# Up-projection of a transformer trunk in seven products: their order, their PSUM banks and what is tied behind the bank reads

## The chip, the cores and the metric

The kernel runs on one core of one Trainium2 chip. The metric is the device time of one execution in microseconds, smaller is better; a time given for a kernel is the median of its runs. PE is the matrix engine, PEld its weight loads, DVE the vector engine, ACT the scalar (activation) engine, POOL the GpSimd engine, SP the engine that issues almost all DMAs. Each engine takes its instructions strictly in order.

## The reference, cut to what matters

```
h = rmsnorm(x, norm_ffn[l]) * (1.0 + sc_f) + sh_f
gate, up = jnp.split(h @ w_up[l], 2, axis=-1)
x = x + g_f * ((jax.nn.silu(gate) * up) @ w_down[l])
```

This is the feed-forward part of the one layer, all in fp32; x is 2048 tokens by 1024, w_up is 1024 by 2 x 2816. Before it stand the mixer with its in- and out-projection, after it the last RMSNorm. The change touches the product `h @ w_up` and the `silu(gate) * up` on its results.

## The kernel before, in words

Every matrix product is done on fp32 operands that are split into a high and a low part (`split`, L151 and L152): ACT casts the high part, DVE subtracts it from the source to get the low one. One product of a 128x128 weight tile and 512 tokens then is three matmuls (`mm3`, L173 to L175).

The up-projection takes tokens in two halves b of 1024, and the 22 units of 128 gate and 128 up columns in 11 pairs. That makes 22 passes, called pairs here. For one unit and one token half the product is a 2x2 block product (gate and up columns by two halves of the contraction, times two token quarters of 512), which is done by Strassen's method in Winograd's form: seven products P1 to P7 in place of eight. Each of the seven has a left operand (A11, A12, A22 of the weights, or the sums S1 to S4 of them, `LEFT`) and a right one (B11, B21, B22, or the sums T1 to T4 of the activations, `RIGHT`). A product is 4 contraction tiles x 3 matmuls = 12 matmuls per unit, so a pair issues 7 x 2 x 12 = 168, the stage 22 x 168 = 3696.

- **Weights.** `Up.__init__` loads a unit's raw weights in two DMAs (`load_raw`, L158) into a pool of 4 slots, so two units fill it. `Up.weights` splits A11, A12, A22 into slots w (6) and S1 to S4 into slots x (4); the sums are made on POOL in place (L571, L572, L575, L581).
- **Activations.** The right operands of one token half stand split in 14 panel slots; those of the second half are loaded and split during the last pair of the first half (`Panel`, L534).
- **Banks.** PSUM has eight banks, a ring of one tag. A unit takes four of them: a (P1, then P2 added on it), d (P5, then P3), b (P6), c (P7, then P4). A pair thus goes once around the ring. The partial sums are read midway: ACT copies a after P1 (u, L604); DVE adds b to u (L607), c to u and d to that (c22, L611 and L612) after P7, before P4 goes onto c; Silu reads a after P2 (L616); then g1 (L620, L621) and c22 (L624, L626) are finished.
- **Results.** Four result blocks of a pair are combined on POOL (L637 to L646) and stored to DRAM (`put` in `sums`, L634) for the down-projection.
- **Background.** In the first token half `ffn_inputs` makes the activations of the second half (POOL, ACT, DMAs), in the second half `down_sums` makes the sums of the down weights (loads L498, POOL L507 to L515, stores L502).

The order on each engine is set by a scheduler that sends out what is ready by the order of the code; a load or store stands on SP at the place the scheduler gave it, and a store that waits for its data holds all loads behind it. `tc.issue_after(ins)` lets instructions be placed only behind `ins`.

Of the kernel before, what the change touches and what calls it, by code (L numbers as in the profile page):

```python
# [13 lines left out]
P = 128  # L14
# [8 lines left out]
NB = 2  # L23
# [19 lines left out]
def trunk_kernel(  # L43
# [408 lines left out]

    def ffn_inputs(b):


        def put(name, kt, t):
            nc.sync.dma_start(hd[b][name][:, kt, :], t)

        def get(i, kt):
            t = tmp(f"b_{b}_{i}_{kt}")  # L460
            nc.sync.dma_start(t, xd[b][kt // 2][:, 2 * (kt % 2) + i, :])
            nc.gpsimd.tensor_mul(t, t, rs[i])  # L462
            nc.scalar.activation(
                t, t, AF.Identity, bias=mod[:, 24 + kt:25 + kt], scale=gain[:, 1, kt:kt + 1]
            )
            return t

        rs = [tmp(f"r_{b}_{i}") for i in range(QB)]
        for i in range(QB):
            nc.sync.dma_start(rs[i], rd[b][i])  # L470
        yield
        for kt in range(4):
            b11 = get(0, kt)
            put("B11", kt, b11)
            t1 = get(1, kt)
            yield
            nc.gpsimd.tensor_sub(t1, t1, b11)
            put("T1", kt, t1)
            t2 = get(1, kt + 4)
            put("B22", kt, t2)  # L480
            yield
            nc.gpsimd.tensor_sub(t2, t2, t1)
            put("T2", kt, t2)
            b21 = get(0, kt + 4)
            put("B21", kt, b21)
            yield
            nc.gpsimd.tensor_sub(b11, t2, b11)
            put("T3", kt, b11)
            nc.gpsimd.tensor_sub(b21, b21, t2)
            put("T4", kt, b21)  # L490
            yield

    def down_sums():

        def get(p, name):
            t = tmp(f"{name}_d{p}")
            u = U_FF + 3 * (2 * p + int(name[2]) - 1) + 2
            nc.sync.dma_start(t, wts[u][:, 512 * (int(name[1]) - 1):][:, :512])  # L498
            return t

        def put(p, name, t):
            nc.sync.dma_start(sd[p][:, ("S2", "S1", "S4", "S3").index(name), :], t)  # L502

        for p in range(NPR):
            a21, a22, a11 = [get(p, n) for n in ("A21", "A22", "A11")]
            yield
            nc.gpsimd.tensor_add(a21, a21, a22)  # L507
            put(p, "S1", a21)
            nc.gpsimd.tensor_sub(a11, a21, a11)
            put(p, "S2", a11)  # L510
            nc.gpsimd.tensor_sub(a22, a22, a11)
            put(p, "S3", a22)
            a12 = get(p, "A12")
            yield
            nc.gpsimd.tensor_sub(a12, a12, a11)  # L515
            put(p, "S4", a12)
            yield

    ORDER_UP = ("P1", "P2", "P5", "P6", "P7", "P4", "P3")
    ORDER_DOWN = ("P1", "P6", "P7", "P4", "P5", "P3", "P2")

    class Panel:
# [5 lines left out]
        def load(self, name, k):  # L530
            t = panel(f"{name}_{self.b}_{k}", [P, 2, 2, Q])
            for i in range(2):
                raw = tmp(f"raw_{name}_{self.b}_{k}_{i}")
                nc.sync.dma_start(raw, hd[self.b][name][:, 2 * k + i, :])  # L534
                split(t[:, i], raw)
            self.t.setdefault(name, []).extend([t[:, 0], t[:, 1]])

        def steps(self):
            for p in ORDER_UP:
                for k in range(2):  # L540
                    self.load(RIGHT[p], k)
                    yield

        def product(self, p):
            for k in range(2):
                self.load(RIGHT[p], k)

    class Up:
# [18 lines left out]
        def weights(self, p):  # L567
            a11, a12, a21, a22 = self.rg[:, :512], self.rg[:, 512:], self.ru[:, :512], self.ru[:, 512:]
            if p == "P1":
                self.put("A11", a11)  # L570
                nc.gpsimd.tensor_add(a21, a21, a22)  # L571
                nc.gpsimd.tensor_sub(a11, a21, a11)  # L572
            elif p == "P2":
                self.put("A12", a12)
                nc.gpsimd.tensor_sub(a12, a12, a11)  # L575
            elif p == "P5":
                self.put("S1", a21)
            elif p == "P6":
                self.put("S2", a11)
            elif p == "P7":  # L580
                nc.gpsimd.tensor_sub(a21, a22, a11)  # L581
                self.put("S3", a21)
            elif p == "P4":
                self.put("A22", a22)
            else:
                self.put("S4", a12)

        def product(self, p):
            n = f"{self.b}_{self.j}"
            bank = {"P1": "a", "P2": "a", "P5": "d", "P3": "d", "P7": "c", "P4": "c", "P6": "b"}[p]  # L590
            first = p in ("P1", "P5", "P7", "P6")
# [8 lines left out]
            getattr(self, "after_" + p, lambda: None)()  # L600
# [27 lines left out]
    def up(b, t, step, after=lambda p: None):  # L628

        def sums(pair, us):
            def put(name, g):
                nc.sync.dma_start(gd[pair][name][:, b, :], g)  # L634

            (b11, t1), (b21, b22) = [(u.g1, u.c22) for u in us]
            nc.gpsimd.tensor_sub(t1, t1, b11)  # L637
            t2 = tmp(f"t2_{b}_{pair}")
            nc.gpsimd.tensor_sub(t2, b22, t1)
            put("B11", b11)  # L640
            put("B21", b21)
            put("B22", b22)
            put("T1", t1)
            put("T2", t2)
            nc.gpsimd.tensor_sub(b11, t2, b11)
            nc.gpsimd.tensor_sub(b21, b21, t2)  # L646
            put("T3", b11)
            put("T4", b21)

        for pair in range(NPR):  # L650
            us = [Up(b, 2 * pair + k, t) for k in range(2)]
            for p in ORDER_UP:
                for u in us:
                    u.weights(p)
            if pair:
                step()
            for p in ORDER_UP:
                for u in us:
                    u.product(p)
                if pair == NPR - 1:  # L660
                    after(p)
            if pair < NPR - 1:
                sums(pair, us)
        return lambda: sums(pair, us)

    def down(ready):
# [38 lines left out]
        ready()  # L705
# [223 lines left out]
    g = panels[0].steps()  # L929
# [3 lines left out]
    g = ffn_inputs(1)  # L933

    def step():
        finish_rms()
        next(g, None)
        next(g, None)

    ready = up(0, panels[0].t, step, panels[1].product)  # L940
    ready()
    g = down_sums()
    next(g)
    next(g)
    down(up(1, panels[1].t, stepper(g, 4)))
# [62 lines left out]
```

## Time and profile before

| | us |
|---|---|
| runs (3) | 2088.53, 2089.32, 2092.90 |
| median | 2089.32 |
| profiled execution | 2091.01 |
| its span, first to last instruction | 2089.3 |
| PE busy | 1972.1 (94%) |
| DVE busy | 1219.9 (58%) |
| ACT busy | 743.2 (36%) |
| POOL busy | 644.9 (31%) |
| mean granted TensorE clock | 0.974 |

The up-projection stands from 698.4 to 1633.9 us of the span. A matmul that runs at half the clock counts as busy all its time, so 94% busy is not 94% of full speed. The granted clock is 1.00 at 2.4 GHz and 0.50 at 1.2 GHz. Times of the rows are microseconds from the start of the span unless a unit stands with them.

### The profile page before, as it was taken

The page shows a single profiled execution, that of the slowest core. Times are in us where ns is not written, and L with a number is a line of the kernel's source. Part 1 is how long each engine was busy: PE and PEld are TensorE (multiplying, and loading weights), DVE is VectorE, ACT ScalarE, POOL GpSimd, SP SyncE. Part 2 cuts the span into 40 slices and gives each one's busy share as a digit, 9 for nine tenths or more (in the row PEclk, how much of TensorE's full clock was granted, in tenths as well). Part 3 has the DMA queues.
Part 4 walks back from the last instruction along what each step waited for, and adds up shares of the span by engine and source line. Part 5 has one row for each costly group of instructions (what it writes and reads, how often), then busy time and mean ns, then how long its engine had stood idle before and what let it go on. Part 6 is the DMA issues. An engine that isn't in the chain of part 4 may idle for free.

```text
span 2089.3 us, 23165 instructions
## 1 busy us (share of the span) xinstructions
PE 1972.1 (94%) x8424; PEld 1595.7 (76%) x8424; DVE 1219.9 (58%) x1683; ACT 743.2 (36%) x1228; POOL 644.9 (31%) x440
## 2 busy tenths in 40 slices
PE   5999998999999799999999898897999999999996
PEld 3778876888888577888887776786788888888874
DVE  7987677434475656646656764445555464444464
ACT  3431666223474432333334332222232242243321
POOL 3100044012310345466563445555452100010110
PEclk9999999999999899999999999999999999999998
DMA  8467244423456433343435444444343684234432
GB/s 280 169 216 268 101 166 147 133 79 121 156 203 193 153 116 111 138 165 112 143 140 195 137 157 159 155 167 139 122 171 132 262 331 157 91 117 151 136 116 81
DMA packets 136918, 328.23 MB, mean 157 GB/s; under 512 B 14305, under 2 KB 22497, under 8 KB 134498
## 3 DMA queue, kind: packets, MB, share of 16 engines
q1 hardware_dynamic: 136802, 326.74, 45.3%
q8 instruction: 66, 1.08, 0.2%
q14 instruction: 50, 0.41, 0.1%
HBM read 242.28 MB, written 84.41 MB: 156 GB/s over the span
## 4 chain that ended last, share of the span: by engine, by line
PE 63%; DMA 6%; DVE 6%; issue 3%; POOL 3%; ACT 2%; SPq 1%; DVEq 0%; POOLq 0%; ACTq 0%
PE d_P L174 7%; PE d_P L173 6%; PE d_P L175 6%; PE gu_c L173 3%; PE gu_c L174 3%; PE gu_c L175 3%; PE gu_d L174 3%; PE gu_d L173 3%; PE gu_d L175 3%; PE gu_a L173 2%; PE gu_a L175 2%; PE gu_a L174 2%; DMA raw_gu<-in_wts 2%; PE c L173 2%; PE c L175 2%
## 5 line engine op out<-in xcount | busy, mean ns | idle before, releaser
L152 DVE TENSOR_TENSOR A<-raw_gu,A 128x512 fp32r<-128x512 f32 x132 | 128.2, 994 | 228.7 <-ACT A L151 228.2
L152 DVE TENSOR_TENSOR ws<-raw_gu,ws 128x512 fp32r<-128x512 f32 x176 | 171.5, 1008 | 38.9 <-ACT ws L151 36.6
L151 ACT CAST A<-raw_gu 128x512 fp32r<-128x512 f32 x132 | 79.2, 618 | 276.7 <-PE gu_c L175 203.3
L151 ACT CAST ws<-raw_gu 128x512 fp32r<-128x512 f32 x176 | 102.4, 619 | 184.4 <-PE gu_d L175 67.9
L173 PE MATMUL gu_a<-B,A 128*128 128x512 f32 x352 | 138.9, 395 | 15.4 <-ACT u L604 15.4
L175 PE MATMUL gu_a<-B,A 128*128 128x512 f32 x352 | 138.2, 393 | 0.0
L174 PE MATMUL gu_a<-B,A 128*128 128x512 f32 x352 | 137.9, 392 | 0.0
L175 PE MATMUL c<-h,w_c 128*128 128x512 f32 x320 | 125.7, 393 | 4.8 <-DVE w_c L152 4.8
L133 POOL TENSOR_TENSOR sf<-sf,sq 128x512 f32<-128x512 f32 x18 | 28.3, 1576 | 328.7 <-ACT sq L132 327.7
L173 PE MATMUL c<-h,w_c 128*128 128x512 f32 x320 | 126.1, 394 | 0.7 <-DVE ya L301 0.7
L174 PE MATMUL c<-h,w_c 128*128 128x512 f32 x320 | 125.5, 392 | 0.3 <-DVE h L224 0.3
L173 PE MATMUL gu_c<-T,A 128*128 128x512 f32 x176 | 76.8, 436 | 42.8 <-DVE c L611 42.7
L637 POOL TENSOR_TENSOR c<-c,g 128x512 f32<-128x512 f32 x22 | 29.3, 1332 | 265.2 <-DVE c L626 265.2
L571 POOL TENSOR_TENSOR raw_gu<-raw_gu 128x512 f32<-128x512 f32 x44 | 61.8, 1405 | 153.3 <-DMA raw_T<-hd_T 99.9
L173 PE MATMUL d_P<-T_d,S_d 128*128 128x512 f32 x264 | 102.7, 389 | 0.0
L174 PE MATMUL d_P<-T_d,S_d 128*128 128x512 f32 x264 | 102.7, 389 | 0.0
L175 PE MATMUL d_P<-T_d,S_d 128*128 128x512 f32 x264 | 102.7, 389 | 0.0
L462 POOL TENSOR_TENSOR b<-b,r 128x512 f32<-128x512 f32 x32 | 41.7, 1318 | 178.5 <-DMA b<-xd 143.9
L133 POOL TENSOR_TENSOR sx<-sx,sq 128x512 f32<-128x512 f32 x14 | 21.0, 1499 | 233.2 <-ACT sq L132 232.3
L173 PEld LDWEIGHTS gu_a<-B,A 128*128 128x128 f32 x352 | 66.7, 190 | 30.7 <-ACT u L604 16.4
L152 DVE TENSOR_TENSOR S_d<-raw_S_d,S_d 128x512 fp32r<-128x512 f32 x44 | 32.1, 734 | 93.8 <-ACT S_d L151 87.1
L173 PEld LDWEIGHTS gu_c<-T,A 128*128 128x128 f32 x176 | 36.9, 209 | 55.8 <-DVE c L611 47.5
(256 smaller groups left out, 5642.1 us busy)
## 6 DMA issues: line engine op xcount, KB each, us to landing
raw_gu<-in_wts SPq DMA_DIRECT2D x88, 512.0 KB, 4.8
raw_T_d<-gd_T SPq DMA_DIRECT2D x44, 512.0 KB, 4.1
raw_B_d<-gd_B SPq DMA_DIRECT2D x33, 512.0 KB, 3.4
wm<-in_wmodT SPq DMA_DIRECT2D x32, 512.0 KB, 4.3
raw_o<-in_wts SPq DMA_DIRECT2D x32, 512.0 KB, 5.5
raw_c<-in_wts SPq DMA_DIRECT2D x28, 512.0 KB, 4.0
gd_B<-g SPq DMA_DIRECT2D x44, 256.0 KB, 2.0
gd_T<-g SPq DMA_DIRECT2D x44, 256.0 KB, 2.0
```

The source lines that it names most:

```text
L133: (add or nc.vector).tensor_add(acc, acc, sq)
L151: nc.scalar.copy(dst[:, 0, :], src)
L152: (sub or nc.vector).tensor_sub(dst[:, 1, :], src, dst[:, 0, :].bitcast(F32))
L173: nc.tensor.matmul(ps, l_hi, r_hi, start=start, stop=False, skip_group_check=onto)
L174: nc.tensor.matmul(ps, l_hi, r_lo, start=False, stop=False, skip_group_check=onto)
L175: nc.tensor.matmul(ps, l_lo, r_hi, start=False, stop=stop, skip_group_check=onto)
L462: nc.gpsimd.tensor_mul(t, t, rs[i])
L571: nc.gpsimd.tensor_add(a21, a21, a22)
L637: nc.gpsimd.tensor_sub(t1, t1, b11)
```

## The change

The seven products come in the order P1, P5, P6, P2, P7, P3, P4, with the operands and matmuls as they were. A unit takes three banks: a (P1, P6, P7 and P4 added onto one another), d (P5, P3) and e (P2). Each partial sum is read between two products onto its bank: ACT copies a after P1 (s), d after P5 (c22), a after P6 (u); DVE adds e to s after P2 and a to c22 after P7; d is added to u after P3, and a is multiplied by s after P4.

The raw loads of the next pair stand in one block; its splits are tied, by `issue_after`, behind the bank read of the current pair's product, one product later than their own place, and the last ones (A22) behind the pair's own P1. Stores of results, of the activations' and the weights' sums are collected (`Late`, `Pair.stores`) and tied behind the last load issued. The panels of the second half are loaded four blocks at a time and split one product later. The steps of the background work come after P6 and P3 of each pair.

```diff
+    class Late:
+        def put(self, dst, t):
+            self.stores.append((dst, t))
+        def flush(self):
+            with tc.issue_after(last["load"]):
+                for dst, t in self.stores:
+                    nc.sync.dma_start(dst, t)
+            self.stores = []
...
-    ORDER_UP = ("P1", "P2", "P5", "P6", "P7", "P4", "P3")
+    ORDER_UP = ("P1", "P5", "P6", "P2", "P7", "P3", "P4")
...
         def steps(self):
             for p in ORDER_UP:
-                for k in range(2):
-                    self.load(RIGHT[p], k)
-                    yield
+                self.load(RIGHT[p])
+                yield
+                self.split(RIGHT[p])
+                yield
...
-            bank = {"P1": "a", "P2": "a", "P5": "d", "P3": "d", "P7": "c", "P4": "c", "P6": "b"}[p]
-            first = p in ("P1", "P5", "P7", "P6")
+            bank = {"P5": "d", "P3": "d", "P2": "e"}.get(p, "a")
+            first = p in ("P1", "P5", "P2")
...
         def after_P1(self):
-            self.u = tmx(f"u_{self.b}_{self.j}")[:, :Q]
-            nc.scalar.copy(self.u, self.ps["a"])
+            self.s, ins = self.copy("s", "a")
+            return ins
+        def after_P5(self):
+            self.c22, ins = self.copy("c22", "d")
+            return ins
         def after_P6(self):
-            nc.vector.tensor_add(self.u, self.ps["b"], self.u)
+            self.u, ins = self.copy("u", "a")
+            return ins
+        def after_P2(self):
+            nc.vector.tensor_add(self.s, self.ps["e"], self.s)
+            return nc.scalar.activation(self.s, self.s, AF.Silu).ins
         def after_P7(self):
-            self.c22 = tmx(f"c22_{self.b}_{self.j}")[:, :Q]
-            nc.vector.tensor_add(self.c22, self.ps["c"], self.u)
-            nc.vector.tensor_add(self.c22, self.ps["d"], self.c22)
-        def after_P2(self):
-            self.s = tmp(f"s1_{self.b}_{self.j}")
-            nc.scalar.activation(self.s, self.ps["a"], AF.Silu)
-        def after_P4(self):
-            self.g1 = tmp(f"g1_{self.b}_{self.j}")
-            nc.vector.tensor_add(self.g1, self.ps["c"], self.u)
-            nc.vector.tensor_mul(self.g1, self.g1, self.s)
+            return nc.vector.tensor_add(self.c22, self.ps["a"], self.c22).ins
         def after_P3(self):
             nc.vector.tensor_add(self.u, self.ps["d"], self.u)
             nc.scalar.activation(self.u, self.u, AF.Silu)
-            nc.vector.tensor_mul(self.c22, self.c22, self.u)
+            return nc.vector.tensor_mul(self.c22, self.c22, self.u).ins
+        def after_P4(self):
+            return nc.vector.tensor_mul(self.s, self.ps["a"], self.s).ins
...
+    def ups(panels, begin, backgrounds):
+        todo = [(b, p) for b in range(NB) for p in range(NPR)]
+        pair, before = begin, None
+        for n, (b, p) in enumerate(todo):
+            after = Pair(*todo[n + 1], panels[todo[n + 1][0]].t) if n + 1 < len(todo) else None
+            bg = backgrounds[b]
+            due = pair.due
+            for k, prod in enumerate(ORDER_UP):
+                ins = pair.product(prod)
+                with tc.issue_after(ins):
+                    if k == 0 and due:
+                        pair.weights(due)
+                    if k and after:
+                        after.weights(ORDER_UP[k - 1])
+                if p == NPR - 1 and b + 1 < NB:
+                    if k:
+                        panels[b + 1].split(RIGHT[ORDER_UP[k - 1]])
+                    panels[b + 1].load(RIGHT[prod])
+                elif p == 0 and b and k == 0:
+                    panels[b].split(RIGHT[ORDER_UP[-1]])
+                if before:
+                    if k == 0:
+                        before.sums()
+                    if k == 3:
+                        with tc.issue_after(last["load"]):
+                            before.stores()
+                    if k == 5:
+                        with tc.issue_after(last["load"]):
+                            before.last_stores()
+                if k in (2, 5):
+                    next(bg, None)
+            if after:
+                after.due = ORDER_UP[-1]
...
```

**PE, the first pair.** On PE the first pair (units 0 and 1 of the first token half) stands before as follows; of each product's twelve matmuls the first is shown, gu0_1_a is bank a of unit 1.

```order
L173 MATMUL gu0_1_a_5490<-B11_0_0_4698,A11_0_1_5434 128x512
...
L173 MATMUL gu0_0_a_5475<-B21_0_0_4822,A12_0_0_5439 128x512
...
L173 MATMUL gu0_1_a_5490<-B21_0_0_4822,A12_0_1_5443 128x512
...
L173 MATMUL gu0_0_b_5559<-T2_0_0_5010,ws_0_0_0_5447 128x512
...
L173 MATMUL gu0_1_c_5603<-T3_0_0_5102,ws_0_1_1_5462 128x512
...
L173 MATMUL gu0_0_c_5587<-T4_0_0_5196,A22_0_0_5465 128x512
...
L173 MATMUL gu0_1_c_5603<-T4_0_0_5196,A22_0_1_5468 128x512
...
L173 MATMUL gu0_0_d_5533<-B22_0_0_5290,ws_0_0_1_5458 128x512
```

And now:

```order
L173 MATMUL gu0_1_a_5498<-B11_0_0_4774,A11_0_1_5434 128x512
...
L173 MATMUL gu0_0_d_5513<-T1_0_0_4868,ws_0_0_0_5439 128x512
...
L173 MATMUL gu0_1_d_5528<-T1_0_0_4868,ws_0_1_0_5443 128x512
...
L173 MATMUL gu0_0_a_5483<-T2_0_0_4962,ws_0_0_0_5439 128x512
...
L173 MATMUL gu0_0_a_5483<-T3_0_0_5148,ws_0_0_1_5459 128x512
...
L173 MATMUL gu0_1_a_5498<-T3_0_0_5148,ws_0_1_1_5462 128x512
...
L173 MATMUL gu0_0_d_5513<-B22_0_0_5242,ws_0_0_1_5459 128x512
...
L173 MATMUL gu0_0_a_5483<-T4_0_0_5336,A22_0_0_5469 128x512
```

P2 (A12 with B21) followed P1 onto bank a, and P4 (A22 with T4) followed P7 onto bank c, each with only the twelve matmuls of the other unit between the two on one bank. Now P5 stands between P1 and P6 on bank a, and P3 between P7 and P4.

**SP, the loads of a pair of the second half.** Units 6 and 7 are the fourth pair of the second token half; raw_gu are their raw weights, gd result stores, A21_d and the like loads of down weights, sd the stores of their sums. Before:

```order
L158 DMA raw_gu1_6_0_9517<-in_wts 128x1024
L158 DMA raw_gu1_6_1_9519<-in_wts 128x1024
L634 DMA gd_1_T1_77<-c22_1_2_9134 128x512
...
L634 DMA gd_1_T3_79<-g1_1_2_9165 128x512
...
L498 DMA A21_d2_9279<-in_wts 128x512
...
L502 DMA sd_2_145<-A21_d2_9279 128x512
L502 DMA sd_2_145<-A11_d2_9283 128x512
...
L502 DMA sd_2_145<-A12_d2_9291 128x512
...
L498 DMA A11_d3_9299<-in_wts 128x512
L158 DMA raw_gu1_7_0_9521<-in_wts 128x1024
L158 DMA raw_gu1_7_1_9523<-in_wts 128x1024
```

And now:

```order
L465 DMA sd_1_144<-A21_d1_9050 128x512
L465 DMA sd_1_144<-A11_d1_9054 128x512
L158 DMA raw_gu1_6_0_9207<-in_wts 128x1024
L158 DMA raw_gu1_6_1_9209<-in_wts 128x1024
L158 DMA raw_gu1_7_0_9211<-in_wts 128x1024
L158 DMA raw_gu1_7_1_9213<-in_wts 128x1024
L465 DMA sd_1_144<-A22_d1_9052 128x512
L465 DMA sd_1_144<-A12_d1_9174 128x512
L674 DMA gd_1_B11_73<-s_1_2_8946 128x512
...
L674 DMA gd_1_T3_79<-s_1_2_8946 128x512
```

Between the loads of unit 6 and those of unit 7 stood sixteen rows, stores of results and of sums among them. Now the four stand together, behind two stores of sums; the other stores come after them.

**ACT, from P1 of that pair on.** Units 8 and 9 are the next pair. Before:

```order
L151 CAST A11_1_8_9819<-raw_gu1_8_0_9811 128x512
L604 COPY u_1_6_9608<-gu1_6_a_9595 128x512
L604 COPY u_1_7_9623<-gu1_7_a_9610 128x512
L616 ACTIVATE s1_1_6_9637<-gu1_6_a_9595 128x512
L616 ACTIVATE s1_1_7_9651<-gu1_7_a_9610 128x512
L151 CAST A11_1_9_9824<-raw_gu1_9_0_9815 128x512
L151 CAST A12_1_8_9829<-raw_gu1_8_0_9811 128x512
L151 CAST A12_1_9_9833<-raw_gu1_9_0_9815 128x512
```

And now:

```order
L628 COPY s_1_6_9510<-gu1_6_a_9497 128x512
L628 COPY s_1_7_9525<-gu1_7_a_9512 128x512
L151 CAST A22_1_6_9527<-raw_gu1_6_1_9209 128x512
L151 CAST A22_1_7_9530<-raw_gu1_7_1_9213 128x512
L628 COPY c22_1_6_9549<-gu1_6_d_9536 128x512
L628 COPY c22_1_7_9564<-gu1_7_d_9551 128x512
L151 CAST A11_1_8_9566<-raw_gu1_8_0_9489 128x512
L151 CAST A11_1_9_9571<-raw_gu1_9_0_9493 128x512
L628 COPY u_1_6_9588<-gu1_6_a_9497 128x512
L628 COPY u_1_7_9602<-gu1_7_a_9512 128x512
L151 CAST ws_1_8_0_9604<-raw_gu1_8_1_9491 128x512
L151 CAST ws_1_9_0_9608<-raw_gu1_9_1_9495 128x512
```

ACT copied bank a once per unit, behind one cast of the next pair, and the Silu of P2 followed. Now it copies three times per unit, and the copies u after P6 stand behind the two casts A11 of the next pair's weights.

## Rows read from the trace of the kernel before

**Rows 1.** Windows: start:end us, length, busy us (x) per engine, clock, DMA share, GB/s.
```profile
core 0: us, PE busy (x) PEld busy (x) DVE busy (x) ACT busy (x) POOL busy (x), PEclk, DMA share, GB/s
698.39:1633.94 935.55, 877.29 (x3705) 706.52 (x3703) 540.34 (x666) 289.44 (x501) 479.47 (x333) 0.96 0.41 143
844.00:1076.00 232.00, 232.00 (x1007) 188.38 (x1006) 139.78 (x168) 76.39 (x132) 137.76 (x96) 1.00 0.39 139
719.43:725.20 5.77, 5.76 (x14) 4.52 (x15) 2.06 (x3) 3.10 (x5) 2.44 (x2) 0.50 0.36 105
1147.87:1151.90 4.03, 4.03 (x10) 3.20 (x11) 4.03 (x6) 0.00 (x0) 1.28 (x1) 0.50 0.48 171
755.55:758.98 3.43, 3.43 (x10) 1.52 (x8) 2.91 (x5) 3.15 (x5) 1.46 (x2) 1.00 0.95 357
```

**Rows 2.** Waits of PE, the whole run: us in total, times, longest.
```profile
PE gu_c L173 <- DVE c L611: 42.7, 9, 7.5
PE gu_a L173 <- ACT u L604: 15.4, 1, 15.4
```

**Rows 3.** Waits of PE in the second token half, 1155 to 1634 us.
```profile
PE gu_c L173 <- DVE c L611: 33.6, 7, 7.5
```

**Rows 4.** Chain of waits ending 1290 us: start us, us, what (pair 3, second half).
```profile
1254.29 1.29 POOL g L646
...
1265.09 1.76 POOL A_d L515
1266.87 0.32 SPq L502
...
1268.26 5.62 DMA raw_gu<-in_wts
...
1282.90 0.61 DVE c L611
```

**Rows 5.** Timeline of SP, same stretch: start us, us, engine line op.
```profile
1246.88 0.94 SPq L158 DMA_DIRECT2D raw_gu<-in_wts  x2
...
1262.09 5.10 SPq L502 DMA_DIRECT2D sd<-A_d  x4
```

**Rows 6.** Page, DMA issues: count, KB each, median us to landing.
```profile
raw_gu<-in_wts SPq DMA_DIRECT2D x88, 512.0 KB, 4.8
```

**Rows 7.** Lines of DVE, 698 to 1634 us: busy us, mean ns | idle before.
```profile
L152 DVE TENSOR_TENSOR ws<-raw_gu,ws 128x512 fp32r<-128x512 f32 x175 | 170.8, 1009 | 33.9 <-ACT ws L151 31.6
...
L612 DVE TENSOR_TENSOR c<-gu_d,c 128x512 f32<-128x512 f32 x44 | 30.4, 691 | 1.4
...
L611 DVE TENSOR_TENSOR c<-gu_c,u 128x512 f32<-128x512 f32 x44 | 30.0, 682 | 10.1 <-PE gu_c L175 10.1
```

**Rows 8.** Lines of ACT, same stretch.
```profile
L604 ACT COPY u<-gu_a 128x512 f32<-128x512 f32 x44 | 25.2, 584 | 28.8 <-PE gu_a L175 28.8
```

**Rows 9.** Chain of waits ending 722 us: the first pair's start.
```profile
703.25 0.63 ACT ws L151
...
715.70 1.88 DVE B L152 x3
717.58 0.67 DVE x L431
...
718.28 0.63 ACT sq L439
718.91 0.48 ACT u L604
...
719.43 0.80 PE gu_a L173
```

**Rows 10.** Chain of waits ending 1150 us: last pair of the first half.
```profile
1123.82 4.89 DMA raw_B<-hd_B
1128.72 6.54 DMA raw_T<-hd_T
...
1144.33 2.88 DVE T L152 x4
```

More of the change, by code (lines that the diff above doesn't have):

```diff
@@ L491, in ffn_inputs @@
             yield
+            late.flush()
     def down_sums():
+        late = Late()
         def get(p, name):
@@ L528, in __init__, with load, split @@
             self.b, self.t = b, {}
[L530 to L536, printed above, removed]
+        def load(self, name):
+            self.raw = []
+            for kt in range(4):
+                raw = tmp(f"raw_{name}_{self.b}_{kt}")
+                nc.sync.dma_start(raw, hd[self.b][name][:, kt, :])
+                self.raw.append(raw)
+        def split(self, name):
+            self.t[name] = hi_lo_views(f"{name}_{self.b}", 4)
+            for kt in range(4):
+                split(self.t[name][kt], self.raw[kt])
         def steps(self):
             for p in ORDER_UP:
-                for k in range(2):
-                    self.load(RIGHT[p], k)
[L542 to L546, printed above, removed]
+                self.load(RIGHT[p])
+                yield
+                self.split(RIGHT[p])
+                yield
     class Up:
@@ L625, in after_P3 @@
             nc.scalar.activation(self.u, self.u, AF.Silu)
-            nc.vector.tensor_mul(self.c22, self.c22, self.u)
[L628 to L636, printed above, removed]
-            nc.gpsimd.tensor_sub(t1, t1, b11)
[L638 to L664, printed above, removed]
@@ L666, in down, with __init__, weights, product @@
-    def down(ready):
+            return nc.vector.tensor_mul(self.c22, self.c22, self.u).ins
+        def after_P4(self):
+            return nc.vector.tensor_mul(self.s, self.ps["a"], self.s).ins
+    class Pair:
+        def __init__(self, b, p, t):
+            self.b, self.p = b, p
+            self.us = [Up(b, 2 * p + k, t) for k in range(2)]
+        def weights(self, prod):
+            for u in self.us:
+                u.weights(prod)
+        def product(self, prod):
+            for u in self.us:
+                ins = u.product(prod)
+            return ins
+        def put(self, name, g):
+            nc.sync.dma_start(gd[self.p][name][:, self.b, :], g)
+        def sums(self):
+            (b11, t1), (b21, b22) = [(u.s, u.c22) for u in self.us]
+            nc.gpsimd.tensor_sub(t1, t1, b11)
+            self.t2 = tmp(f"t2_{self.b}_{self.p}")
+            nc.gpsimd.tensor_sub(self.t2, b22, t1)
+        def stores(self):
+            (b11, t1), (b21, b22) = [(u.s, u.c22) for u in self.us]
+            for name, g in (("B11", b11), ("B21", b21), ("B22", b22), ("T1", t1), ("T2", self.t2)):
+                self.put(name, g)
+            nc.gpsimd.tensor_sub(b11, self.t2, b11)
+            nc.gpsimd.tensor_sub(b21, b21, self.t2)
+        def last_stores(self):
+            self.put("T3", self.us[0].s)
+            self.put("T4", self.us[1].s)
@@ new lines, in ups @@
+    def ups(panels, begin, backgrounds):
[31 more added lines that the diff above has]
+                after.due = ORDER_UP[-1]
+            if p == NPR - 1:
+                for _ in bg:
+                    pass
+            before, pair = pair, after
+        return before
@@ L669, in down @@
+    def down(last_pair):
         x, ps = [[] for _ in range(NB)], {}
@@ L704, in down @@
         early = {("P1", p): (left("P1", p), right("P1", p)) for p in range(3)}
-        ready()
+        last_pair.sums()
+        last_pair.stores()
+        last_pair.last_stores()
         for prod in ORDER_DOWN[:-1]:
@@ L932, in trunk_kernel, with inputs @@
         pass
-    g = ffn_inputs(1)
-    def step():
-        finish_rms()
[L937 to L945, printed above, removed]
+    first = Pair(0, 0, panels[0].t)
+    for prod in ORDER_UP:
+        first.weights(prod)
+    first.due = None
+    def inputs():
+        finish_rms()
+        yield from ffn_inputs(1)
+    down(ups(panels, first, [inputs(), down_sums()]))
 def _columns(a):
```

38 lines of the change are left out of this document (25 added, 13 removed).

## The prediction

> **What bounds the kernel now.** I first read the table of windows, to see at what speed PE works in the up-projection. The stage lasts 935.55 us [rows 1]. In six of its pairs, 844 to 1076 us, PE is busy for all of 232.00 us at a granted clock of 1.00: 1007 matmuls, so 0.2304 us each and 38.7 us a pair. All 3696 matmuls at that pace are 851.5 us; the stage lies 84.1 us above it. Then the waits of PE, which name most of that: 42.7 us in nine waits of bank c's next product for the DVE read L611, and one wait of 15.4 us of bank a for the ACT copy L604 [rows 2], together 58.1 us. Both are reads of a partial sum before the next product goes onto the same bank. The matmuls of the RMSNorm row sums take 3.43 us for ten, of which two are ordinary: 3.0 us more [rows 1]. The rest, 84.1 - 58.1 - 3.0 = 23.0 us, is half speed after the waits: right behind two of them the granted clock is 0.50, and 14 matmuls take 5.77 us in place of 3.23 (2.5 lost), ten take 4.03 in place of 2.30 (1.7 lost) [rows 1]. Spread over ten waits it is 2.3 us each, which fits the two rows.
>
> Then I read the chains of waits, for what made the reads late. In the second half seven of the nine waits stand, 33.6 us [rows 3]. Their chain [rows 4] starts with POOL's last result sum, goes through POOL's sums of down weights and a store of these on SP, and reaches the raw load of the pair's second unit only at 1268.26; the DVE read of bank c ends at 1283.51. On SP the loads of the first unit were issued at 1246.88, and four stores that waited for POOL held the queue for 5.10 us from 1262.09 [rows 5]. So the cause is the loads' place in the queue, and DVE's read suffers since it stands behind splits that wait for these loads. In the last pair of the first half the chain is the same with panel loads, 4.89 and 6.54 us, and four T splits ahead of the read [rows 10]. In the first pair ACT's copy stands behind its casts and a square that waits for DVE's x, itself behind three splits of B22 [rows 9].
>
> **The change part by part.** *The cover of each read.* Before, only the other unit's twelve matmuls, 12 x 0.2304 = 2.8 us, lay between a product on bank a or c and the next one on it. Now it is a whole product of both units, 5.5 us, for every read. The DVE read of bank a after P7 is one add of 0.68 us [rows 7] for each unit, where two stood before; P7 ends at 5 x 5.53 = 27.6 us of the pair and P4 starts at 33.2, so behind both adds (1.4 us) 4.2 us are left, more than one split at its mean of 1.01 us, or two.
>
> *The loads.* A pair's four loads now stand together and the stores are tied behind them. They can start when the raw slots come free, with the low parts of A22, which is split after P1 of the pair before: by about 5.5 us, four casts of 0.63 [rows 9] and two subtractions at 1.0 [rows 7] no later than 10 us. A load takes 4.8 us in the median [rows 6], 5.62 in the chain above [rows 4]: there by 15.6. Two casts and two copies of 0.58 [rows 8] later, at 18.0, u is copied; P7 needs it at 4 x 5.53 = 22.1. I leave 4 us of slack, and cost this edit at nothing: the cover is P2, from 16.6 to 22.1. If the cover is gone, it is the slower rival below.
>
> *The work of the engines.* ACT gets two copies more per unit, 88 x 0.58 = 51 us, DVE loses two adds of 0.69, 88 x 0.69 = 61 us [rows 7, 8]. In the clean stretch DVE is busy for 139.78 of 232 us, POOL for 137.76, ACT for 76.39 [rows 1]; ACT goes to about 90 of 232. Neither is near its limit, so this is worth nothing by itself.
>
> *The waits of bank c* go, all nine. The one place where I leave something is the last pair of the first half: 28 panel splits still stand in front of the same reads, over some eight products or 44 us. DVE's own 23.3 us a pair there (139.78 / 6), less 2.8 for the four adds gone, and 28 splits at the 0.72 of [rows 10] (2.88 / 4) make 40.6; at 1.01 us a split, beside POOL, 48.8. So from 0 to 5 us of overrun, and with a wait of the next pair and a restart up to 11. I take 3, near the lower end, since the row of T splits itself shows 0.72.
>
> *The start.* P5 now runs where PE stood for 15.4 us. It needs only S1, whose casts end about 704 [rows 9], and fresh banks: 24 x 0.2304 = 5.5 us. Then P6 waits for ACT's copies of bank a. In ACT's order they still stand behind the square of x, which in turn waits for the DVE add L431 at 717.58 and ends at 718.91; the copy ends at 719.39 [rows 9]. P1 had ended 15.4 us before 719.43, at 704.0, so P5 ends at 709.5, and 9.9 us of wait are left, with a restart of 2.5. Bounds: nothing left, if the DVE add comes out earlier (the three B22 splits before it fall behind it), and 15.4 if P5 is late too. I take 9.9.
>
> *The sum.* The stage after: 851.5 + 3.0 + 9.9 + 2.5 = 866.9 us, 68.7 less than 935.55. From the profiled execution, 2091.01 (1.7 us above its span's 2089.3), that makes 2022.3, with the 3 of the seam 2025.3. That execution lies 1.7 us above the median of the runs, 2089.32. Forecast: 2024 us.
>
> On the clock, the profile shows 0.50 after each wait of 4 us and more that I looked at [rows 1], and I book 20.5 us of the gain on it. The Trainium skill (TensorE: Matmul & The Clock Gate, part 1, the HAM clock gate) advises to model the ramp as under 1% of a span and to fit no count of cold matmuls; the row's 23.0 us are 1.1% of this span, and without this term the time would be 2044.
>
> **The rivals.** *Loads still late in the second half.* The block of four loads stands behind stores of down-weight sums that wait for POOL, as in the chain [rows 4]. If they land late as before, DVE's and ACT's in-order queues carry the delay to the reads, cover or not. Then the seven waits of the second half stay: 33.6 us and 7 x 2.3 = 16.1, together 50, so 2074; with the 5.5 us of cover against 2.8, which takes up to 2.7 us from each, half of it, about 2050. For it: the sums of POOL are there as before. Against: before, sixteen rows stood between a pair's loads, now none. The Trainium skill (the same page, HAM oscillation) tells of a kernel that waited on DMA in which more buffering in PSUM brought no further gain; by that rule this rival is the outcome, at its full 2074.
>
> *The start's wait goes as well.* If the DVE add L431 comes earlier, 9.9 + 2.5 go too, and the time is 2012.
>
> *Half speed isn't given back.* PE may fall to 0.50 in the stage without a wait that the profile lists; against it the six clean pairs at 1.00. It would be 2044.
>
> *The order moves nothing:* PE waits for what is late in any order, DMA or POOL, and the time stays at 2089. Against it: the two lines that PE waited for are reads of DVE and ACT, and the clean pairs show that all engines keep up with 38.7 us.
>
> *Slower: ACT's copies behind the next pair's casts.* u is now copied behind the casts A11 of the next pair, and these wait for raw loads. As worked out, u is there at 18.0 and wanted at 22.1; it decides when a load takes over 9.7 us from issue to landing in place of 4.8. Then every pair but the last waits for the excess and restarts at half speed: with 1 us of excess (1.0 + 2.3) x 21 = 69, the whole gain, and 2093; with 2 us 2114. For it: a wait of this kind didn't exist before, DMA issues queue on one SP. Against: the longest landings in the chains are 5.62 and 6.54 us [rows 4, 10].
>
> **How the numbers follow.** Forecast 0.56, in its own range 2015 to 2035. Second-half loads late 0.20 (2045 to 2075). Start gone too 0.08. Half speed not regained 0.05. No change 0.04. Slower 0.05; two seams and the start leave 0.02 unnamed, half of them slower. All of these but no change, slower and half of the unnamed are over 0.2% (4.2 us, what a measurement of this kernel can tell from no change) faster: 0.90 faster, 0.04 the same, 0.06 slower. The range 2010 to 2056 leaves out the late loads in their worse half (0.09), no change and slower, some 0.2 in all.
>
> **What would show it.** Right: the windows of the stage give about 867 us, PE has no wait on L647, the DVE read after P7, nor on the copies but for the first pair's of about 10 us; all pairs of the second half take 38.7 us at a granted clock of 1.00. The raw loads of a pair are issued within 10 us of its predecessor's start and in one block. Wrong: waits of PE in the second half whose chain again passes through a store on SP and a raw load (first rival); PE waiting for the copy u in most pairs with a cast A11 ahead of it (slower); a clock under 1.00 in pairs without a wait.

## The result and the profile after

The changed kernel takes 2030.11 us in the median of four runs (2028.27 to 2034.65), the kernel before 2089.78; the ratio is 0.9715, with a 95% interval of 0.9696 to 0.9735. The forecast was 2024, the range 2010 to 2056. The profiled execution after took 2028.27 us, its span 2026.3.

The table of windows of the changed kernel: the whole up-projection, its second token half, and the stretches behind three waits (columns as in [rows 1]).

```profile
core 0: us, PE busy (x) PEld busy (x) DVE busy (x) ACT busy (x) POOL busy (x), PEclk, DMA share, GB/s
698.00:1570.00 872.00, 861.59 (x3705) 697.23 (x3705) 475.16 (x575) 334.65 (x587) 469.60 (x332) 0.99 0.45 152
1144.10:1570.00 425.90, 425.90 (x1849) 346.63 (x1848) 233.01 (x277) 154.66 (x273) 239.15 (x169) 1.00 0.50 171
...
943.20:948.20 5.00, 4.93 (x22) 4.09 (x23) 3.23 (x7) 2.00 (x4) 2.93 (x2) 1.00 0.00 0
781.70:786.70 5.00, 4.98 (x15) 3.93 (x16) 3.24 (x6) 2.06 (x4) 2.91 (x2) 0.66 0.00 0
712.70:718.40 5.70, 5.70 (x14) 4.46 (x15) 2.53 (x4) 3.05 (x6) 1.28 (x1) 0.50 0.69 228
```

The stage is 63.6 us shorter than the 935.55 of [rows 1]; the whole span fell by 63.0. In the second half PE is busy all the time at full clock: 425.90 us for 1849 matmuls, 0.2303 each. Its busy time over the stage fell by 15.7 us (877.29 to 861.59) for as many matmuls; most of that is half clock given back. In the trace before, the granted clock is 0.50 behind each of the eight waits of 3.96 us and more; half of PE's busy time there, some 19 us, is lost. Behind the two short waits, 0.66 and 0.40 us, it stays at 1.00. In the trace after it is 0.50 twice, behind the wait at the start and from 783.2 to 786.6; that loses 4.6 us. A short wait of the kernel before, and the second stretch after (columns as above):

```profile
1236.80:1241.80 5.00, 4.95 (x22) 4.08 (x23) 3.84 (x6) 0.62 (x1) 1.78 (x2) 1.00 0.00 0
```

```profile
783.20:786.60 3.40, 3.40 (x9) 2.63 (x8) 1.64 (x4) 1.96 (x4) 2.65 (x2) 0.50 0.00 0
```

The waits of PE in the stage, from the view of the whole run:

```profile
PE gu_a L173 <- DVE c L647: 7.0, 6, 1.8
...
PE gu_a L173 <- ACT s L628: 3.4, 1, 3.4
```

The 58.1 us of [rows 2] are 10.4 now. But L647, the read of bank a after P7, for which I expected no wait, has six, all in the first token half. The chain of waits that ends with one of them (start us, us, what):

```profile
928.69 1.75 POOL s L687
930.45 0.32 SPq L674
...
930.82 3.86 DMA b<-xd
...
934.75 1.30 POOL b L478
936.06 1.29 POOL b L478
...
937.38 0.82 ACT b L479
938.19 0.51 ACT A L151
...
939.24 1.56 ACT ws L151 x3
...
940.84 1.77 DVE ws L152
942.61 0.61 DVE c L647
...
943.27 0.50 PE gu_a L173
```

Read from the top: POOL's last result sum lets a tied result store go, behind which SP holds a load of the second half's inputs; POOL scales what has landed, ACT activates it (L479), and behind that, on ACT, stand the next pair's casts A12 and S2; the subtractions of S2 stand on DVE ahead of the read. (A12's split is tied to this very read, L647; its subtraction does stand behind it on DVE, at 943.73, but its casts on ACT went ahead.)

### The profile page after: what moved, and what is told of

Read it like the earlier page. It is cut to its first block, busy times and chain, and to the rows that moved or that the text cites. A ratio compares the mean times of both kernels' runs of the same rounds, so it can differ in the third digit from the quotient of the medians.

```text
span 2026.3 us, 23006 instructions
## 1 busy us (share of the span) xinstructions
PE 1956.1 (97%) x8424; PEld 1585.4 (78%) x8424; DVE 1156.8 (57%) x1595; ACT 787.6 (39%) x1314; POOL 636.3 (31%) x440
## 4 chain that ended last, share of the span: by engine, by line
PE 68%; DMA 4%; DVE 4%; POOL 3%; issue 2%; ACT 2%; SPq 0%; DVEq 0%; POOLq 0%; ACTq 0%
PE d_P L174 7%; PE d_P L175 7%; PE d_P L173 7%; PE gu_a L173 7%; PE gu_a L174 6%; PE gu_a L175 6%; DMA raw_gu<-in_wts 3%; PE gu_d L173 3%; PE gu_d L174 3%; PE gu_d L175 3%; PE c L173 2%; PE c L174 2%; PE c L175 2%; PE o L175 1%; PE gu_e L175 1%
## 5 line engine op out<-in xcount | busy, mean ns | idle before, releaser
L152 DVE TENSOR_TENSOR ws<-raw_gu,ws 128x512 fp32r<-128x512 f32 x176 | 197.3, 1159 | 158.7 <-ACT ws L151 150.7
L152 DVE TENSOR_TENSOR A<-raw_gu,A 128x512 fp32r<-128x512 f32 x132 | 101.3, 799 | 122.4 <-ACT A L151 121.5
L173 PE MATMUL gu_a<-T,ws 128*128 128x512 f32 x352 | 140.3, 399 | 3.4 <-ACT s L628 3.4
L174 PE MATMUL gu_a<-T,ws 128*128 128x512 f32 x352 | 140.0, 398 | 0.0
L175 PE MATMUL gu_a<-T,ws 128*128 128x512 f32 x352 | 139.8, 397 | 0.0
L478 POOL TENSOR_TENSOR b<-b,r 128x512 f32<-128x512 f32 x32 | 42.2, 1334 | 182.4 <-DMA b<-xd 156.9
L173 PEld LDWEIGHTS gu_a<-T,ws 128*128 128x128 f32 x352 | 66.6, 189 | 20.1 <-ACT s L628 3.9
L174 PEld LDWEIGHTS gu_a<-T,ws 128*128 128x128 f32 x352 | 66.7, 189 | 16.3
L175 PEld LDWEIGHTS gu_a<-T,ws 128*128 128x128 f32 x352 | 66.5, 189 | 16.4
L151 ACT CAST S_d<-raw_S_d 128x512 fp32r<-128x512 f32 x44 | 27.3, 620 | 131.7 <-PE d_P L175 117.8
```

What stands on the lines that cost most here:

```text
L151: nc.scalar.copy(dst[:, 0, :], src)
L152: (sub or nc.vector).tensor_sub(dst[:, 1, :], src, dst[:, 0, :].bitcast(F32))
L173: nc.tensor.matmul(ps, l_hi, r_hi, start=start, stop=False, skip_group_check=onto)
L174: nc.tensor.matmul(ps, l_hi, r_lo, start=False, stop=False, skip_group_check=onto)
L175: nc.tensor.matmul(ps, l_lo, r_hi, start=False, stop=stop, skip_group_check=onto)
```

## The experiments

Each kernel ran beside the kernel before on the same chip; ratios are to the latter. The stage is from its first matmul to its last; the waits are PE's for reads of banks in the stage. Both are from the one profiled execution of each kernel.

| kernel | us | ratio (95%) | stage | waits |
|---|---|---|---|---|
| order_only | 2030.06 | 0.9723 (0.9709 to 0.9738) | 875.4 | 15.4 |
| ties_only | 2031.15 | 0.9726 (0.9711 to 0.9740) | 874.6 | 15.0 |
| the change | 2030.11 | 0.9715 (0.9696 to 0.9735) | 871.8 | 10.4 |
| stores_untied | 2014.61 | 0.9648 (0.9632 to 0.9664) | 861.9 | 4.5 |
| splits_untied | 2018.21 | 0.9664 (0.9648 to 0.9680) | 863.5 | 5.4 |
| no_ties | 2020.25 | 0.9672 (0.9657 to 0.9686) | 863.6 | 5.8 |
| bg14 | 2021.19 | 0.9677 (0.9661 to 0.9693) | 860.2 | 3.9 |
| order_p4_early | 2087.11 | 0.9995 (0.9983 to 1.0006) | 932.0 | 52.8 |
| after_p4_early | 2089.76 | 1.0005 (0.9992 to 1.0019) | 931.8 | 53.8 |
| untied_p4_early | 2028.00 | 0.9711 (0.9690 to 0.9732) | 872.1 | 12.1 |
| start_p2 | 2013.66 | 0.9644 (0.9624 to 0.9664) | 858.4 | 2.7 |
| splits_start | 2022.85 | 0.9683 (0.9662 to 0.9704) | 865.1 | 6.4 |
| start_bg14 | 2021.34 | 0.9679 (0.9658 to 0.9700) | 866.7 | 7.7 |

**Each half of the change alone.** order_only is the kernel before with the new order, banks and reads:

```diff
-    ORDER_UP = ("P1", "P2", "P5", "P6", "P7", "P4", "P3")
+    ORDER_UP = ("P1", "P5", "P6", "P2", "P7", "P3", "P4")
-            bank = {"P1": "a", "P2": "a", "P5": "d", "P3": "d", "P7": "c", "P4": "c", "P6": "b"}[p]
-            first = p in ("P1", "P5", "P7", "P6")
+            bank = {"P5": "d", "P3": "d", "P2": "e"}.get(p, "a")
+            first = p in ("P1", "P5", "P2")
...
```

> The kernel before with the new product order, banks and mid-bank reads alone; loads, splits, stores and panels stand in its own order, so sixteen rows still lie on SP between the raw loads of a pair's two units in the second half. Theory (loads and reads each carry a part): the two waits of the first half on bank c (9.1 us, with restarts about 14) go, the start loses 6 to 12 us, and the seven waits of the second half (33.6 us, 2.3 of restart each) shrink by the 2.8 us of added cover each, to about 15 us with 7 restarts of 2: 2090 - 14 - 10 - 19 = about 2047, PE waiting for L620-like reads after a late raw load. Rival 1 (only the distance between two products on a bank counts): no wait is left in the second half, about 2030 like the whole change. Rival 2 (only the late loads count): the second half keeps its 33.6 us and restarts, 2066 to 2078.

ties_only is the changed kernel with the old order, banks and reads, the same lines the other way about:

> The whole change but for product order, banks and reads, which are those of the kernel before; a pair's four loads stand together, stores and splits are tied. Theory: with loads in time DVE reads bank c within the 2.8 us, as in pairs 2 to 9 of the kernel before, so the second half has no wait; the start keeps its 15.4 us wait (12 more than the whole change) and the first half gets waits behind the casts that stand on ACT behind the activation of the second half's inputs, now without the 2.8 us of cover: six of 1 to 2 us become six of about 4, with restarts some 30 us more: about 2030 + 12 + 30 = 2072 at most, 2042 if these waits stay as small as now. Rival (the distance between two products on a bank alone decides): the second half waits as before, 2078 to 2090.

Both came out at the time of the whole change: 2030.06 and 2031.15 against 2030.11. So the two halves don't add up; each alone gives the whole gain. For order_only my own theory was wrong (2047) and the first rival had the time right (2030), though not all waits of the second half are gone: 5.9 us are left. ties_only came out better than its theory (2042 to 2072), far from its rival (2078 to 2090). The waits of PE in the second half of order_only, and under them in ties_only:

```profile
PE gu_a L173 <- DVE c L623: 3.7, 2, 2.0
PE gu_a L173 <- ACT u L604: 2.2, 3, 1.0
```

```profile
PE gu_a L173 <- ACT u L628: 1.6, 1, 1.6
```

Yet order_only's loads are nearly as late as before. In the second half the last raw load for the next pair lands 21.0 us into a pair, in the mean of ten; before it was 22.9, in the changed kernel it is 15.2, in ties_only 14.3. The chain of waits of its third pair in the second half:

```profile
1230.35 1.30 POOL A_d L511
1231.64 1.27 POOL A_d L515
...
1232.93 0.32 SPq L502
...
1234.32 5.92 DMA raw_gu<-in_wts
...
1245.82 1.23 DVE ws L152
...
1251.56 1.20 DVE c L623 x2
```

It is the chain of [rows 4] again: a sum of down weights on POOL, its store on SP, the raw load, splits, the read. The first matmuls of P3 and of P4 in that pair, from PE's timeline, and the read from DVE's (idle before and what ended it in brackets):

```profile
1244.84 0.39 PE L173 MATMUL gu_d<-B,ws 128*128 128x512 f32 x1
```

```profile
1252.21 0.50 PE L173 MATMUL gu_a<-T,A 128*128 128x512 f32 x1 [1.61 <-DVE c L623]
```

```profile
1251.48 1.27 DVE L623 TENSOR_TENSOR c<-gu_a,c 128x512 f32<-128x512 f32 x2
```

The first of the two reads ends about 1252.2, 7.3 us after P3 began; only the 1.6 us beyond P3's own time are a wait. Had P4 stood in P3's place, PE should have waited for all of it.

**P4 in P3's place.** That is the next edit, on order_only and later on the changed kernel:

```diff
-    ORDER_UP = ("P1", "P5", "P6", "P2", "P7", "P3", "P4")
+    ORDER_UP = ("P1", "P5", "P6", "P2", "P7", "P4", "P3")
```

> The kernel of order_only with one swap: P4 directly behind P7, P3 last. Bank a is then wanted by P4 one product (5.5 us) earlier after the same read L623, as bank c was in the kernel before; banks, reads, loads and splits as in order_only. Theory (in order_only the reads are as late as before, and the product P3 between P7 and P4 hides it): in order_only the read of the first unit ends after the sixth product's start in 12 of 22 pairs, 43.3 us in all, up to 7.8; these become waits of PE, with 1.7 us of restart or so after each long one: 2030 + 43 + 15 = 2088, not under 2070, and PE waits for L623. Rival (the banks or the ACT copies of the new scheme made the gain, not the place of P3): 2030, no such waits.

> The changed kernel, ties and all, with P4 directly behind P7 and P3 last. In the changed kernel the read of the first unit (L647) ends after the sixth product's start in 13 of 22 pairs, 57.4 us in all. Theory (the tied splits keep the reads late, and the place of P3 alone hides it): these become waits of PE for L647, less what one wait spares the next: 40 to 57 us and 10 to 20 of half clock, 2080 to 2105, the whole gain lost. Rival (early loads suffice, as in ties_only): 2030 to 2045.

Both came out as the theory had them: 2087.11 (forecast 2088) and 2089.76 (2080 to 2105), the time of the kernel before. In these two kernels all of the gain hangs on one swap, although the banks and ACT copies stay, and in the second the early loads and ties too. The waits of the two, order_p4_early first:

```profile
PE gu_a L173 <- DVE c L623: 42.3, 16, 6.5
PE gu_a L173 <- ACT s L604: 6.3, 1, 6.3
PE gu_a L173 <- ACT u L604: 4.2, 2, 2.4
```

```profile
PE gu_a L173 <- DVE c L647: 50.2, 10, 7.3
...
PE gu_a L173 <- ACT s L628: 3.6, 1, 3.6
```

In after_p4_early the loads are early, and the second half hardly waits: 42.5 of the 50.2 us stand in eight waits ahead of 1130 us, in the first half, whose reads the change itself has made late. The ties alone don't do that: in ties_only, which has them with the old order, the first unit's read after P7 starts at most 1.3 us behind its product in the first ten pairs; in the second to the eighth pair it is 0 to 3.1 us in order_only and 7.3 to 9.4 us in the changed kernel. It takes the ties and the new order together.

**The ties.** stores_untied and splits_untied take one kind of tie away, no_ties both:

```diff
-            with tc.issue_after(last["load"]):
+            with nullcontext():
                 for dst, t in self.stores:
...
-                        with tc.issue_after(last["load"]):
+                        with nullcontext():
                             before.stores()
```

```diff
-                with tc.issue_after(ins):
+                with nullcontext():
                     if k == 0 and due:
```

> The changed kernel with the three ties of stores behind the last load taken away; splits stay tied. SP then has T2 and T3 stores between the loads of a pair's units, and result stores ahead of the next pair's loads. Theory: loads come later by the wait for POOL's result sums, up to 5 us, which the 4 us of slack nearly hold: 0 to 20 us slower than the changed kernel, 2030 to 2050, in waits of PE for the copy u or the read L647. Rival (the ties of the stores do the whole second half): seven and more waits of 5 us with restarts come back, about 2075. Rival (they do nothing, block loading is enough): 2030.

> The changed kernel with the splits no longer tied behind the bank reads; loads in a block and stores tied. Theory (the ties of splits keep DVE's and ACT's queues short ahead of the reads): the reads come 1 to 4 us later, mostly within their slack in the second half, but in the first half they are already at the edge: 2030 to 2050. Rival (the ties do nothing, the scheduler puts the splits there anyway): 2030, and L647 with its six waits of 7 us.

> The changed kernel with neither stores nor splits tied; product order, banks, loads in the code of the pair before, panels by four stay. Theory (the gain is in order and early loads, the ties of stores cost, the ties of splits help little): 2015 to 2025. Rival (the split ties are needed where the store ties are gone): waits for L647 or u come back in the second half, 2030 to 2060.

For the first two I was wrong in sign: each is faster than the whole change, by 15.5 and 11.9 us in the medians; no_ties was inside what its theory gave. None of the three has the six waits for L647 (no_ties has one, of 1.4). In the sixth pair, ACT's activations of the inputs stand like this in the changed kernel, where the pair starts at 908.1, and in stores_untied, where it starts at 903.2:

```profile
936.08 0.82 ACT L479 ACTIVATE b<-b,mod,gain 128x512 f32<-128x512 f32 x1 [5.54 <-POOL b L478]
```

```profile
926.71 0.82 ACT L479 ACTIVATE b<-b,mod,gain 128x512 f32<-128x512 f32 x1 [3.34 <-POOL b L478]
```

27.9 us after the pair's start against 23.5. The input loads go at 912.20 there, 9.0 us into the pair, and in the changed kernel at 930.82, 22.7 us into it:

```profile
911.77 0.38 SPq L674 DMA_DIRECT2D gd_T<-s  x1
912.20 1.26 SPq L477 DMA_DIRECT2D b<-xd  x2
```

Of the 13.7 us by which the loads are earlier the activation keeps 4.4; POOL's weight sums (L599 at 922.55) stand ahead of the multiplication (L478 at 925.37).

With the splits untied the stores keep their place in SP's order, and the casts of S2 stand ahead of those activations on ACT (922.53 to 923.67, the activation from 927.38); the read is 1.9 us ahead of P3's start in 13 pairs. But this edit shortens the head of the chain as well. The raw slots come free sooner, so the raw loads, the stores tied behind them and the input loads all go earlier. The input loads stand 12.6 us into the sixth pair, which starts at 905.2:

```profile
917.84 0.95 SPq L477 DMA_DIRECT2D b<-xd  x2
```

So taking away either kind of tie breaks the chain above. What the store's tie does is shown by stores_untied: S2's casts still stand behind the activations there (929.72 behind 927.95), and with these earlier the waits are gone. That the split's tie counts by the place of the casts alone is not shown, since splits_untied changes that place and the loads at once. Why no_ties is no faster than each alone (0.9672 against 0.9648 for stores_untied, with intervals that overlap) I did not settle.

A third edit, meant to break it as well, moves the background steps, with the store ties left:

```diff
-                if k in (2, 5):
+                if k in (1, 4):
                     next(bg, None)
```

> The changed kernel with the background steps after the products P5 and P7 of a pair in place of P6 and P3 (indices 1 and 4 in place of 2 and 5): the loads of the second half's inputs then stand on SP ahead of the result stores that wait for POOL, so that the activations on ACT ahead of the next pair's A12 and S2 casts come earlier. Theory (the six waits of 7.0 us for L647 come from that chain: store of T4 waiting for POOL, input load, POOL, activation, casts, splits): the waits in the first half go, with what they cost in half clock: 7 to 10 us faster, about 2021. Rival (POOL or DVE being full around the read is the cause): no change, 2030. Rival (the early activation now holds up the copy u on ACT): slower, 2035 or more.

The time agrees (2021.19 for 2021), the mechanism does not. Only one of the two activations of a pair comes early; in the sixth pair, which starts at 897.5, the other still stands ahead of S2's casts, 29.8 us into it:

```profile
927.29 0.82 ACT L479 ACTIVATE b<-b,mod,gain 128x512 f32<-128x512 f32 x1 [5.05 <-POOL b L478]
```

The first unit's read ends after P3's start in 14 pairs, 51.5 us in all; in the changed kernel that is 13 pairs and 57.4 us. Four waits for L647 remain, 3.9 us. In the profiled execution (2015.64, the fastest of four by 4.3 us) the first pair's wait is gone too, which the edit was not meant to touch. What makes bg14 faster is open.

untied_p4_early asks whether P3's place still counts when the splits aren't held back; it is the swap above on splits_untied:

> The kernel of splits_untied with the same swap of P3 and P4. There the read L647 ends 1.9 us ahead of the sixth product's start in 13 pairs, 0.5 to 1.6 us ahead in seven, and after it in two, 5.0 us in all. Theory: with splits that go when the loads land, P3's place is hardly needed: 2018 + 5 + 2 = about 2025. Rival (any product order with P4 on P7's heels loses the gain): 2070 or more.

The theory held: 2028.00 for about 2025. Where the reads are in time the swap costs 9.8 us, where they are late 57 to 60.

**The first pair.** Three kernels put P2 ahead of P6 in the first pair, on stores_untied (start_p2), on splits_untied (splits_start), and on start_p2 with the background steps of bg14 (start_bg14):

```diff
+            order = ORDER_UP if n else ("P1", "P5", "P2", "P6", "P7", "P3", "P4")
-            for k, prod in enumerate(ORDER_UP):
+            for k, prod in enumerate(order):
```

> The kernel stores_untied with P2 ahead of P6 in the first pair alone, so that 24 more matmuls (5.5 us, bank e) stand between P1 and P6. Theory (what is left of the stage above its matmuls is the first pair's wait of 4.5 us for the copy of bank a, and its restart of 2.1): the wait is covered, 6 us faster than stores_untied's 2014.6: about 2008. Rival (the copy u after P6 now comes late for P7, which follows it directly, since on ACT it stands behind the casts of the next pair): the wait moves there, 2014 or more.

> The kernel of splits_untied with P2 ahead of P6 in the first pair alone. Theory (all that is left of splits_untied's waits is the first pair's 5.4 us and 2.9 of restart): 8 us faster than its 2018, about 2010; nothing moves to the second pair, since splits there no longer wait behind the activations. Rival (as in start_p2 a wait of 2 to 3 us comes in the second pair): 2013 or more.

> The kernel of start_p2 (stores untied, P2 ahead of P6 in the first pair) with the background steps after indices 1 and 4. Theory (the 2.5 us wait that start_p2 has in the second pair comes from the input's activations ahead of the next splits on ACT): it goes, about 2010. Rival (the second pair's wait is due to its late raw load, 7.1 us): no change, 2014.

All three missed. The wait for the copy s went, and others came: 2.7 us for L647 in start_p2, 6.1 in splits_start, and in start_bg14 6.5 for the copy u, which P7 now follows directly. The waits up to 770 us in start_bg14:

```profile
PE gu_a L173 <- ACT u L628: 6.5, 1, 6.5
PE ms L146 <- ACT sq L439: 1.2, 1, 1.2
```

Moving a read's product forward in one place takes its cover away in another. start_p2 (2013.66, 2011.08 to 2017.12) can't be told from stores_untied (2014.61, 2012.59 to 2016.76); these two are the fastest versions found, some 16 us under the changed kernel.

## Why the prediction was right, and where it was off

The mechanism was the one forecast: all nine waits of bank c went, the second half runs at its floor, and most of the half clock behind the waits came back. Step by step:

- **The cover of each read.** The step that was mis-sized. I wrote "a whole product of both units, 5.5 us, for every read". For the read between P7 and P4 it is 36 matmuls, not 24: the other unit's twelve and P3's 24, 36 x 0.2304 = 8.3 us in place of 2.8. The longest wait before was 7.5 us [rows 2]. So the added 5.5 us hide nearly all lateness whatever its cause, and order_only, late loads and all, shows it; the rival of late loads, 0.20 at about 2050, was priced with 2.7 us of added cover in place of 5.5, and should have stood near 2030. Taking 5.5 us from each of the nine waits leaves 4.9 of the 42.7 us; order_only has 3.7 for this read. Its own theory (2047) had the same 2.8.
- **The loads.** Their early block was right as a fact: forecast to be there by 15.6 us, the last one lands at 15.2 in the mean of the second half, and that half has no wait. But I took it as needed. The half of the change that holds it is one of two remedies that each suffice with the rest as before (ties_only, order_only); which of its parts, early loads, ties or panels, does the work in the old order was not tried. With the new order and P4 early it doesn't suffice (after_p4_early). And the load in the chain of [rows 4] belongs to the next pair, as order_only's does: the reads wait behind splits of weights to come.
- **The waits of bank c.** All nine went, as I wrote, but I had put nothing for new waits in the first half. Behind P7 I had left 4.2 us, "more than one split at its mean of 1.01 us, or two"; in the second to the eighth pair the read starts 7.3 to 9.4 us behind its product. It stands behind S2's subtractions, their casts behind the activations, these behind input loads that follow tied stores. That costs 7.0 us of waits and, behind the first of them, 1.7 of half clock. Taking away ties shortened the profiled stage by 8 to 10 us and the median by 10 to 16; what lies between the two was not taken apart. In the profiled execution the stage came out 2.1 us above the forecast 866.9 and the 3 of the seam. The rest of the 6.1 us between 2024 and the median lies outside the stage and in how far a profiled execution stands from its median: the one before was 1.7 us above, the one after is 1.8 below.
- **The start.** 9.9 us was taken, 3.4 measured. For the order alone 9.9 was right (9.5 in order_only); ties_only, with the old order, has 10.0. Of the old 15.4 either half takes five to six microseconds, and these two gains do add up. What I had as a bound and as a rival (0.08), but not in the sum, is that DVE's x comes earlier. It ended 19.9 us after the stage's start in [rows 9] (717.58 + 0.67, stage from 698.39); now it ends at 13.5:

```profile
710.76 0.74 DVE L431 SCALAR_TENSOR_TENSOR x<-o,mod,x 128x512 f32<-128x512 f32 x1
```

In ties_only it ends 14.5 us after the stage's start, in order_only, whose panels come in the new order too, 19.5. So it is the half with the loads and ties that brings x forward; which part of it is not shown.

- **The seam.** 3 us were taken, none is there: the second half starts at 1144.1 without a wait around it.
- **The clock.** 20.5 us were booked; PE's busy time shows 15.7. The term was too large: I spread 23.0 us over ten waits, but only eight had a restart, some 19 us by the granted clock, and what the rest of the 23.0 is no run shows. One restart behind a new wait, 1.7 us, takes another part. Without the term the sum gave 2044; the 15.7 us speak for keeping it. The Trainium skill (TensorE: Matmul & The Clock Gate, Part 1) puts the ramp under 1% of a typical span. The 19 us are 0.9% of the span before, so the trace agrees with the figure; that it is small is no reason to leave it out where the gain sought is 3%.
- **The rival of late loads at its full price.** The Trainium skill (the same page, HAM oscillation) tells of a kernel whose loop had been rearranged against its DMA waits, and which PSUM double-buffering gave no further gain; what limited it then the page does not say. It does not carry over to this kernel: order_only, with loads nearly as late as before, has the whole gain.
- **The slower rival** (ACT's copies behind the next pair's casts) did not come in the changed kernel: no wait for L628's u. Where the loads are late it did come, but small. order_only has three waits for u, 2.2 us in all, each behind a cast A11 that waited for its raw load; ahead of the one of 1.0 us stands

```profile
1240.26 0.62 ACT L151 CAST A<-raw_gu 128x512 fp32r<-128x512 f32 x1 [7.67 <-DMA raw_gu<-in_wts]
```

The 6.5 us for u in start_bg14 are of another kind: there the copy stands behind the Silu of P2 (730.57), which waited for DVE.

The errors cancel in part: 6.5 us less at the start and 3 at the seam, against the six waits' 7.0 and the 4.8 by which the clock gave back less. That the sum came within 6.1 us of the median is partly luck.

## What to carry to other kernels

Count the matmuls between a read of a bank and the next product on it, per unit and in the order that PE really has; one product more there was worth as much here as the whole half of the change that brings the late loads forward. When two edits each remove the same wait, price them as substitutes, and try each alone: here the half that was not needed brought a new wait. A tie that makes an instruction later needs a look at what stands behind it in each in-order queue, here an input load behind a store on SP and casts behind an activation on ACT.

## What was unexpected of the hardware

Two waits of about the same length, 1.8 and 1.7 us, each after 38 us or more without one, had different ends: behind the one at 781.7 the granted clock of the next 5.0 us was 0.66, behind the one at 943.2 it stayed at 1.00 (15 against 22 matmuls, in the windows of the first table). In order_p4_early the longer wait was the cheaper one: 2.0 us up to 781.1 brought the clock down, 2.8 us up to 1363.0 did not.

```profile
781.10:786.10 5.00, 4.99 (x15) 3.95 (x16) 0.89 (x2) 0.34 (x1) 0.71 (x1) 0.66 0.01 3
1363.00:1368.00 5.00, 5.00 (x22) 4.16 (x23) 1.88 (x3) 0.62 (x1) 0.66 (x1) 1.00 0.09 35
```

What a short wait costs beyond itself can't be read from its length alone.
